# Rotary tables moved from the start into the compressed projections, vector loads on ACT's queue, the last squares summed by a second matmul

## The chip, the core and the metric

The kernel runs on one core of a Trainium2 chip. The metric is the device time of one execution in microseconds. The core has five instruction streams that run side by side and meet at semaphores: TensorE (PE, matmuls; its weight loads are listed as PEld), VectorE (DVE), ScalarE (ACT), GpSimd (POOL) and SyncE (SP), which here only issues transfers. Any of SP, ACT and POOL can issue a DMA; the transfers themselves run on the core's 16 DMA engines.

## What is computed

The reference is an encoder of two layers on 1024 tokens of width 1024. Cut to what the change touches:

```python
cos, sin = rope_tables(positions)         # angles positions * inv_freq: (1024, 16)
c_act = silu(c)
for l in range(2):
    mod = c_act @ w_ada[l] + b_ada[l]     # six rows of 1024: shift, scale, gate, twice
    h = rmsnorm(x, g_mix[l]) * (1 + scale_a) + shift_a
    proj = h @ w_in[l]                    # q_na, k_na, v_na, c_q, c_kv, k_rope, gates
    # neighbourhood attention on q_na, k_na, v_na
    # latent attention on c_q (256), c_kv (128), k_rope (32):
    #   q = rmsnorm(c_q) @ w_uq, its rotary part and k_rope turned by cos and sin
    x = x + gate_a * (merged @ w_out[l])
    h = rmsnorm(x, g_mlp[l]) * (1 + scale_m) + shift_m
    x = x + gate_m * (relu(h @ w_ff1[l]) ** 2 @ w_ff2[l])
return rmsnorm(x, g_final)
```

## The kernel before, in words

The activations lie transposed in SBUF, eight tiles of 128 channels by 1024 tokens, in two halves `ch` of 512 tokens. Every dense product is done as three matmuls: each operand is split into a rounded high part (a cast on ACT, line 201) and the rest (a subtraction on DVE, line 202), and the three products high x high, high x low and low x high add up in PSUM (lines 208 to 210, in the token projections 459 to 461).

The start goes as follows. SyncE loads `c`, the positions, the eight row tiles of `x` (line 132), seven parameter vectors as rows (`load_rows`, line 116), and then sixteen tiles of `w_ada` (line 160), eight for the scale and eight for the shift of layer 0. There are eight completion semaphores for transfers, which are used in turn, and a transfer's issue waits until the earlier one with the same semaphore has landed. DVE computes the rotary tables (lines 302 to 326: angle in turns, split into chunks, reduced modulo one by adding and subtracting a large number in `frac`, lines 309 and 310, and summed in halves at line 319); two sines on ACT (350, 351) finish them into `sinT` and `cosT`, and line 143 loads ACT's usual table again. ACT squares the rows of x (337), POOL makes each row's norm factor out of the sum (338, 339, a power) and a diagonal matrix `dg` of it (342). TensorE turns the rows by a matmul with `dg` (347), and ACT copies the normalised, turned tiles `yT` out (349). DVE sums the ada tiles weighted with `c_act` (line 169 for the first tile, 171 for the others) into `acc1` (scale) and `acc0` (shift). `turn_rows` (123, 124) turns the parameter vectors into columns `cols`; `ada_turn` (185 to 194) adds the sums' partitions up and makes `mod` and `amix`. With these, line 271 modulates `yT`, and after the split the projections begin.

The first projection makes the 416 compressed columns (`c_sink`, 474 to 492, one unit of 24 matmuls for each of eight token tiles) with the norms of `c_q` and `c_kv`; the second the 512 value columns, again eight units. Between value units TensorE does the rotary queries: `query_rot` (line 739) makes 128 tokens x 256 rotary columns `pqr`, `rotate` (380 to 392) turns them on DVE with `sinT` and `cosT` into `qrr`, and one unit later `query_turn` (751) transposes `qrr` on TensorE (756) into `pqrT`. Two token tiles are done after one unit. The scale row of the next modulation, `ada(0, 2)`, is also summed in this stage.

`square_sum` (233) adds up the squares of the eight output tiles while they are made, in the output projection of both layers and in the second product of the channel mixer: ACT squares, DVE adds to `sums`. `rstd_first` (243) sums over partitions with one fp32 matmul with a matrix of ones (245; the trace shows two instructions for it).

The Tile framework builds the program: a scheduler with a model of the engines sets each engine's order, only instructions in `tc.keep_in_program_order` keep theirs. PSUM tiles of one bank come from a pool of four; streamed tiles (`raw`) from a pool of three; `slab` tiles from an arena of 32.

Of the kernel before, what the change touches and what calls it, by code (L numbers as in the profile page):

```python
# [9 lines left out]
F32 = mybir.dt.float32  # L10
# [27 lines left out]
def hybrid_trunk(  # L38
# [42 lines left out]
    def slab(s, shape=(P, 1024), dt=F32):  # L81
        return arena.tile(list(shape), dt, tag="slab", name=nm(s))
# [28 lines left out]
    def load_rows(group, base):  # L111
        t = tmp("vrows", (P, P))
        n = 0
        for name, ap, cnt in group:
            flat = ap if len(ap.shape) == 1 else ap.rearrange("a b -> (a b)")
            nc.sync.dma_start(t[n:n + cnt, :], flat.rearrange("(r p) -> r p", p=P))
            col0[name] = base + n
            n += cnt
        return t, n
# [5 lines left out]

    tc_, nc_ = load_rows(rows_c, 248)
    pint = tmp("pi", (8, P), I32)
    nc.sync.dma_start(pint, positions.rearrange("a (i p) -> (a i) p", p=P))
    xrow = []
    for i in range(8):  # L130
        t = slab("xrow")
# [10 lines left out]
    def exp_ln_tables():  # L142
        tc.keep_in_program_order(A.preload_act_table_set("natural_log_exp_and_others"))
# [54 lines left out]
        nc.sync.dma_start(dst.bitcast(F32), src.bitcast(F32))  # L198

    def split(dst_hi, dst_lo, src, pin=lambda ins: ins):  # L200
        pin(A.copy(dst_hi, src))  # L201
        V.tensor_tensor(dst_lo, src, dst_hi.bitcast(F32), op=ALU.subtract)  # L202

    def mm3(ps, terms, first=True, **kw):

# [22 lines left out]

    pipe = Pipe()

    sums = [None, None]

    def square_sum(src, ch, n):

        if n == 0:
            sums[ch] = pool["ws"].tile([P, CH], F32, tag=f"sums{ch}", name=nm("sums"), bufs=1)
            A.activation(sums[ch], src, AF.Square)
        else:
            sq = tmp("sq")
            A.activation(sq, src, AF.Square)  # L240
            V.tensor_tensor(sums[ch], sums[ch], sq, op=ALU.add)

    def rstd_first(ch):
        ps = bank("pss")
        T.matmul(ps, ones, sums[ch], start=True, stop=True)
        v = tmp("var")
        V.tensor_scalar(v, ps, 1.0 / D, EPS, op0=ALU.mult, op1=ALU.add)
        r0 = tmp("r0")
        A.activation(r0, v, AF.Ln)
        A.activation(r0, r0, AF.Exp, scale=-0.5)  # L250
        return v, r0
# [43 lines left out]
        V.memset(invf[:, i:i + 1], f)  # L295

    dense_open()
    n, chunks, magic = P, turn_chunks(), 1.5 * 2.0 ** 23
    turns, rest = (pool["ws"].tile([P, 2048], F32, tag="ws", name=s) for s in ("turns", "rest"))
    ang, parts = rest[:, 1792:1920], rest[:, 1536:1792]  # L300
    for i in range(8):
        V.tensor_scalar(ang[:, i * 16:(i + 1) * 16], invf, posT[:, i:i + 1], None, op0=ALU.mult)
    ahi = parts[:, n:]
    V.tensor_copy(ahi.bitcast(F32R), ang)
    V.tensor_tensor(parts[:, :n], ang, ahi, op=ALU.subtract)

    def frac(t):
        w = rest[:, :t.shape[1]]
        V.tensor_scalar(w, t, magic, magic, op0=ALU.add, op1=ALU.subtract)
        V.tensor_tensor(t, t, w, op=ALU.subtract)  # L310

    m = 2 * n * len(chunks)
    for i, cval in enumerate(chunks):
        V.tensor_scalar(turns[:, 2 * n * i:2 * n * (i + 1)], parts, cval, None, op0=ALU.mult)
    frac(turns[:, :m])
    frac(turns[:, :m])
    while m > n:
        half = m // n // 2 * n
        V.tensor_tensor(turns[:, :half], turns[:, :half], turns[:, m - half:m], op=ALU.add)
        frac(turns[:, :half])  # L320
        m -= half
    two_pi = 2.0 * math.pi * (1 - 2.0 ** -22)
    flat = lambda t: t[:].rearrange("p a b -> p (a b)")
    turn, quarter = turns[:, :n], turns[:, n:2 * n]
    V.tensor_scalar(quarter, turn, 0.25, None, op0=ALU.add)
    frac(quarter)


    x_d = dram.tile([D, S], F32, name="x_d")
# [13 lines left out]
    for ch in range(2):  # L343
        for k in range(8):
# [2 lines left out]
                T.matmul(ps[:, i * P:(i + 1) * P], xrow[4 * ch + i][:, k * P:(k + 1) * P], dg[ch][:, i, :],  # L347
                         start=True, stop=True)
            A.copy(yT[k][:, cs(ch)], ps)
    tc.keep_in_program_order(A.activation(flat(sinT), turn, AF.Sin, scale=two_pi))  # L350
    tc.keep_in_program_order(A.activation(flat(cosT), quarter, AF.Sin, scale=two_pi))
    exp_ln_tables()
    pin = tc.keep_in_program_order
    ada_sum(acc1, first_scale, 0, pin)
    ada_sum(acc0, first_shift[:5], 0, pin)
    turn_rows(ta, na_, 0)
# [92 lines left out]
    def projections(l, h, xs, mla, extra, behind, early):  # L449
# [24 lines left out]
        def c_sink(i, ps):  # L474
# [12 lines left out]
                pipe.later(1, mla["key_copy"], ctok, i // 2)  # L487
            if i in (4, 5, 6, 7):
                vws.extend(token_weights(l, 1024, 512, [i - 4], pin=tc.keep_in_program_order))
            if i == 3:  # L490
                for k in range(8):
                    nc.sync.dma_start(x_d[k * P:(k + 1) * P, :], xs[k])
# [482 lines left out]
    def layer(l, xs, h, extra, behind, early):  # L975
# [61 lines left out]

        def operand_h(p, k, src):
            t = hq[p, k] = pair_slab("h")
            split(t[:, 0, :], t[:, 1, :], src)  # L1040

        def scaled(ch, r, ks):
            for k in ks:
# [462 lines left out]
def turn_chunks():  # L1506

    from fractions import Fraction

    digits = "0.1591549430918953357688837633725143620344596457404564487476673440588967976342265350901138027662530859560728"  # L1510
    rest = Fraction(digits)
    got = []
    for _ in range(6):
        e = math.floor(math.log2(float(rest)))
        step = Fraction(2) ** (e - 11)
        c = (rest / step).__floor__() * step
        got.append(float(c))
        rest -= c
    return got
# [26 lines left out]
```

## Time and profile before

| | us |
|---|---|
| median of 3 runs (3151.32 to 3154.35) | 3153.73 |
| the profiled execution | 3154.83 |
| its span, first to last instruction | 3153.0 |
| TensorE busy (96%) | 3033.6 |
| VectorE busy (66%) | 2069.4 |
| ScalarE busy (47%) | 1471.2 |
| GpSimd busy (12%) | 373.0 |

The shares are of the span. TensorE's mean granted clock is 0.988 of full speed. Matmuls are pipelined, so that a recorded duration overlaps the next; the step from start to start tells what one costs in a run of them. An "idle before" in a row is the time that the engine did nothing ahead of that instruction, and the name behind the arrow is what came last before it could start.

### The profile page before, as it was taken

Reading aid. Unit: us, or ns where it says so; the run is one execution under the profiler, and the core shown is the slowest. Engines: PE = TensorE matmul, PEld = TensorE weight load, DVE = VectorE, ACT = ScalarE, POOL = GpSimd, SP = SyncE. Lnnn points to the kernel's source line nnn. Section 1 sums busy time; section 2 is a strip of 40 time slices with the busy share of each in tenths; the row PEclk is TensorE's granted clock in tenths of the full one; section 3 lists DMA queues with packets and bytes.
Section 4 is the critical chain, followed back from the end, with each engine's and each line's share of the span. In section 5 each row is a group of like instructions: output and inputs, shape, how many; then the busy total and the mean of one; then the engine's idle time right before and its main releaser. Section 6 shows DMA issues by size and latency. Waiting matters only on the chain. (4 is left out here: it accounts for less than half of the span.)

```text
span 3153.0 us, 43333 instructions
## 1 busy us (share of the span) xinstructions
PE 3033.6 (96%) x15104; PEld 2456.0 (78%) x15104; DVE 2069.4 (66%) x3911; ACT 1471.2 (47%) x2820; POOL 373.0 (12%) x518
## 2 busy tenths in 40 slices
PE   7999999999998999999989999999999999999998
PEld 6878886776786888888777788777777778888887
DVE  8534436767859776877774334466775697767775
ACT  6234446554127666433352444555522466663332
POOL 5111002232200000000011011123221000000000
PEclk9999999999999999999999999999999999999999
DMA  6554334214853656856334444431266255586652
GB/s 258 157 135 111 99 109 119 63 36 145 280 191 107 244 207 231 293 196 209 106 121 138 125 121 114 117 86 36 73 214 218 69 180 214 211 308 205 215 166 84
DMA packets 359540, 497.56 MB, mean 158 GB/s; under 512 B 30556, under 2 KB 238618, under 8 KB 359322
## 3 DMA queue, kind: packets, MB, share of 16 engines
q1 hardware_dynamic: 359322, 494.80, 48.9%
q8 instruction: 119, 1.95, 0.3%
q14 instruction: 99, 0.81, 0.1%
HBM read 335.41 MB, written 141.98 MB: 151 GB/s over the span
## 5 line engine op out<-in xcount | busy, mean ns | idle before, releaser
L208 PE MATMUL pd<-h,wh 128*128 128x512 f32 x768 | 307.0, 400 | 0.6 <-ACT wh L201 0.6
L210 PE MATMUL pd<-h,wh 128*128 128x512 f32 x768 | 300.7, 392 | 0.0
L209 PE MATMUL pd<-h,wh 128*128 128x512 f32 x768 | 300.1, 391 | 0.0
L208 PE MATMUL pxz<-ho,wq 128*128 128x512 f32 x672 | 259.9, 392 | 3.5 <-DVE xT L1401 3.0
L209 PE MATMUL pxz<-ho,wq 128*128 128x512 f32 x672 | 261.8, 390 | 0.5 <-DVE ho L1153 0.5
L210 PE MATMUL pxz<-ho,wq 128*128 128x512 f32 x672 | 257.0, 389 | 0.0
L201 ACT CAST wq<-s 128x512 fp32r<-128x512 f32 (+3 forms) x296 | 154.5, 541 | 125.5 <-PE pxz L210 54.2
L208 PE MATMUL px<-h,wq 128*128 128x512 f32 x512 | 202.2, 396 | 3.5 <-ACT u L1242 2.3
L1401 DVE SCALAR_TENSOR_TENSOR xT<-pxz,mod,xT 128x512 f32<-128x512 f32 x252 | 186.7, 744 | 28.4 <-PE pxz L210 28.3
L798 DVE TENSOR_REDUCE sm<-smla 128x1 f32<-128x1024 f32 x128 | 156.6, 1223 | 69.7 <-PE smla L796 63.3
L209 PE MATMUL px<-h,wq 128*128 128x512 f32 x512 | 200.2, 392 | 1.4 <-DVE h L202 1.4
L210 PE MATMUL px<-h,wq 128*128 128x512 f32 x512 | 199.6, 391 | 0.0
L801 ACT ACTIVATE pmla<-smla,sm 128x1024 f32<-128x1024 f32 x128 | 143.0, 1117 | 118.2 <-DVE sm L799 113.3
L803 POOL TENSOR_SCALAR pmla<-pmla,sm 128x1024 f32<-128x1024 f32 x128 | 144.6, 1130 | 330.4 <-DVE sm L799 153.7
L202 DVE TENSOR_TENSOR wq<-s,wq 128x512 fp32r<-128x512 f32 (+3 forms) x296 | 168.7, 582 | 6.9 <-ACT wq L201 6.9
L796 PE MATMUL smla<-st,st 128*128 128x512 f32 x512 | 170.4, 413 | 2.9 <-ACT pmla L801 2.9
L208 PEld LDWEIGHTS pd<-h,wh 128*128 128x128 f32 x768 | 144.9, 189 | 32.4 <-issue 3.4
L210 PEld LDWEIGHTS pd<-h,wh 128*128 128x128 f32 x768 | 144.6, 188 | 32.8 <-issue 1.0
L209 PEld LDWEIGHTS pd<-h,wh 128*128 128x128 f32 x768 | 145.1, 189 | 28.3
L201 ACT CAST wq<-wr 128x384 fp32r<-128x384 f32 (+3 forms) x218 | 114.7, 539 | 106.2 <-PE pxz L210 62.6
L209 PE MATMUL pyz<-h,wq 128*128 128x512 f32 x384 | 151.6, 395 | 8.0 <-DVE h L202 8.0
L208 PEld LDWEIGHTS pxz<-ho,wq 128*128 128x128 f32 x672 | 126.1, 188 | 36.3 <-issue 4.8
(281 smaller groups left out, 7344.3 us busy)
## 6 DMA issues: line engine op xcount, KB each, us to landing
hid_d<-diff SPq DMA_DIRECT2D x112, 512.0 KB
ho<-hid_d SPq DMA_DIRECT2D x112, 512.0 KB
wada<-in_w_ada_dram SPq DMA_DIRECT2D x96, 512.0 KB
wr<-in_w_ff_dram SPq DMA_DIRECT2D x64, 512.0 KB
w<-in_w_in_dram SPq DMA_DIRECT2D x56, 512.0 KB
wr<-in_w_ff_dram SPq DMA_DIRECT2D x64, 384.0 KB
ho<-hid_d SPq DMA_DIRECT2D x84, 256.0 KB
hid_d<-u SPq DMA_DIRECT2D x68, 256.0 KB
```

The lines of the kernel that those rows point to most:

```text
L201: pin(A.copy(dst_hi, src))
L202: V.tensor_tensor(dst_lo, src, dst_hi.bitcast(F32), op=ALU.subtract)
L208: T.matmul(ps, wh, mh, start=first and i == 0, stop=False, **kw)
L209: T.matmul(ps, wh, ml, start=False, stop=False, **kw)
L210: T.matmul(ps, wl, mh, start=False, stop=i == n - 1, **kw)
L796: T.matmul(ps[:, cs(ch)], a[:, t], b[:, cs(ch)], start=i == 0, stop=i == 2)
L798: V.reduce_max(sm[:, 0:1], ps, axis=AX.X)
L801: A.activation(pt, ps, AF.Exp, bias=sm[:, 1:2], scale=MLA_SCALE, accum_out=sm[:, 2:3])
L803: G.tensor_scalar(pt, pt, sm[:, 3:4], 1.0, op0=ALU.mult, op1=ALU.mult)
L1401: V.scalar_tensor_tensor(x, ps, gate_m[:, nt:nt + 1], x, op0=ALU.mult, op1=ALU.add)
```

## The change

- The eight loads of vectors and the load of the positions are issued by ACT instead of SyncE.
- The rotary tables are computed in a function `rotary_tables()`, called in the first layer's compressed projection at its fifth unit instead of at the start. The work tiles are three slabs, and the chunks are worked in two halves of 768 columns instead of one of 1536. The first eight operations and the two sines keep their place in the program's order.
- In `square_sum` the last of the eight squares isn't added by DVE; `rstd_first` adds it by a second matmul into the same PSUM tile.
- `split` and `operand_h` return their instructions.

```diff
@@ -113,7 +113,7 @@
         n = 0
         for name, ap, cnt in group:
             flat = ap if len(ap.shape) == 1 else ap.rearrange("a b -> (a b)")
-            nc.sync.dma_start(t[n:n + cnt, :], flat.rearrange("(r p) -> r p", p=P))
+            nc.scalar.dma_start(t[n:n + cnt, :], flat.rearrange("(r p) -> r p", p=P))
@@ -125,7 +125,7 @@
 
     tc_, nc_ = load_rows(rows_c, 248)
     pint = tmp("pi", (8, P), I32)
-    nc.sync.dma_start(pint, positions.rearrange("a (i p) -> (a i) p", p=P))
+    nc.scalar.dma_start(pint, positions.rearrange("a (i p) -> (a i) p", p=P))
@@ -198,8 +198,8 @@
         nc.sync.dma_start(dst.bitcast(F32), src.bitcast(F32))
 
     def split(dst_hi, dst_lo, src, pin=lambda ins: ins):
-        pin(A.copy(dst_hi, src))
-        V.tensor_tensor(dst_lo, src, dst_hi.bitcast(F32), op=ALU.subtract)
+        a = pin(A.copy(dst_hi, src))
+        return a, V.tensor_tensor(dst_lo, src, dst_hi.bitcast(F32), op=ALU.subtract)
@@ -228,7 +228,7 @@
-    sums = [None, None]
+    sums, last_sq = [None, None], [None, None]
@@ -238,11 +238,15 @@
         else:
             sq = tmp("sq")
             A.activation(sq, src, AF.Square)
-            V.tensor_tensor(sums[ch], sums[ch], sq, op=ALU.add)
+            if n < 7:
+                V.tensor_tensor(sums[ch], sums[ch], sq, op=ALU.add)
+            else:
+                last_sq[ch] = sq
 
     def rstd_first(ch):
         ps = bank("pss")
-        T.matmul(ps, ones, sums[ch], start=True, stop=True)
+        T.matmul(ps, ones, sums[ch], start=True, stop=False)
+        T.matmul(ps, ones, last_sq[ch], start=False, stop=True)
         v = tmp("var")
         V.tensor_scalar(v, ps, 1.0 / D, EPS, op0=ALU.mult, op1=ALU.add)
         r0 = tmp("r0")
@@ -295,35 +299,45 @@
...
-    n, chunks, magic = P, turn_chunks(), 1.5 * 2.0 ** 23
-    turns, rest = (pool["ws"].tile([P, 2048], F32, tag="ws", name=s) for s in ("turns", "rest"))
-    ang, parts = rest[:, 1792:1920], rest[:, 1536:1792]
-    for i in range(8):
-        V.tensor_scalar(ang[:, i * 16:(i + 1) * 16], invf, posT[:, i:i + 1], None, op0=ALU.mult)
-    ahi = parts[:, n:]
-    V.tensor_copy(ahi.bitcast(F32R), ang)
-    V.tensor_tensor(parts[:, :n], ang, ahi, op=ALU.subtract)
-
-    def frac(t):
...
-    for i, cval in enumerate(chunks):
-        V.tensor_scalar(turns[:, 2 * n * i:2 * n * (i + 1)], parts, cval, None, op0=ALU.mult)
-    frac(turns[:, :m])
-    frac(turns[:, :m])
...
+    def rotary_tables():
+
+        n, chunks, magic = P, turn_chunks(), 1.5 * 2.0 ** 23
+        ta, tb, tw = (slab(s) for s in ("turns", "turns", "rest"))
+        parts, ang = tw[:, 768:1024], ta[:, 896:1024]
+        for i in range(8):
+            pin(V.tensor_scalar(ang[:, i * 16:(i + 1) * 16], invf, posT[:, i:i + 1], None, op0=ALU.mult))
+        ahi = parts[:, n:]
+        V.tensor_copy(ahi.bitcast(F32R), ang)
+        V.tensor_tensor(parts[:, :n], ang, ahi, op=ALU.subtract)
+
+        def frac(t):
+            w = tw[:, :t.shape[1]]
+            V.tensor_scalar(w, t, magic, magic, op0=ALU.add, op1=ALU.subtract)
+            V.tensor_tensor(t, t, w, op=ALU.subtract)
+
+        m = n * len(chunks)
+        for t, cut in ((ta, chunks[:len(chunks) // 2]), (tb, chunks[len(chunks) // 2:])):
+            for i, cval in enumerate(cut):
+                V.tensor_scalar(t[:, 2 * n * i:2 * n * (i + 1)], parts, cval, None, op0=ALU.mult)
+            frac(t[:, :m])
+            frac(t[:, :m])
+        V.tensor_tensor(ta[:, :m], ta[:, :m], tb[:, :m], op=ALU.add)
+        frac(ta[:, :m])
+        while m > n:
+            half = m // n // 2 * n
+            V.tensor_tensor(ta[:, :half], ta[:, :half], ta[:, m - half:m], op=ALU.add)
+            frac(ta[:, :half])
+            m -= half
+        two_pi = 2.0 * math.pi * (1 - 2.0 ** -22)
+        turn, quarter = ta[:, :n], ta[:, n:2 * n]
+        V.tensor_scalar(quarter, turn, 0.25, None, op0=ALU.add)
+        frac(quarter)
+        pin(A.activation(flat(sinT), turn, AF.Sin, scale=two_pi))
+        pin(A.activation(flat(cosT), quarter, AF.Sin, scale=two_pi))
+        exp_ln_tables()
...
@@ -347,10 +361,6 @@
                 T.matmul(ps[:, i * P:(i + 1) * P], xrow[4 * ch + i][:, k * P:(k + 1) * P], dg[ch][:, i, :],
                          start=True, stop=True)
             A.copy(yT[k][:, cs(ch)], ps)
-    tc.keep_in_program_order(A.activation(flat(sinT), turn, AF.Sin, scale=two_pi))
-    tc.keep_in_program_order(A.activation(flat(cosT), quarter, AF.Sin, scale=two_pi))
-    exp_ln_tables()
-    pin = tc.keep_in_program_order
     ada_sum(acc1, first_scale, 0, pin)
     ada_sum(acc0, first_shift[:5], 0, pin)
     turn_rows(ta, na_, 0)
@@ -487,6 +497,8 @@
                 pipe.later(1, mla["key_copy"], ctok, i // 2)
             if i in (4, 5, 6, 7):
                 vws.extend(token_weights(l, 1024, 512, [i - 4], pin=tc.keep_in_program_order))
+            if i == 4 and l == 0:
+                rotary_tables()
@@ -1037,7 +1049,7 @@
 
         def operand_h(p, k, src):
             t = hq[p, k] = pair_slab("h")
-            split(t[:, 0, :], t[:, 1, :], src)
```

DVE at the start, before: `ada_43` is the shift's sum, `ada_42` the scale's (its last row stands first), `cols` the turned vectors.

```order
L171 SCALAR_TENSOR_TENSOR ada_42_233<-wada_33_215,c_act_114,ada_42_233 128x1024
L169 TENSOR_SCALAR ada_43_234<-wada_34_217,c_act_114 128x1024
L171 SCALAR_TENSOR_TENSOR ada_43_234<-wada_35_219,c_act_114,ada_43_234 128x1024
L124 COPY cols_81<-pcols_62_382 128x112
L124 COPY cols_81<-pcols_63_385 128x62
L171 SCALAR_TENSOR_TENSOR ada_43_234<-wada_36_221,c_act_114,ada_43_234 128x1024
L187 TENSOR_REDUCE mod0_118<-pada_64_388 128x4
L187 TENSOR_REDUCE mod0_118<-pada_65_394 128x4
L171 SCALAR_TENSOR_TENSOR ada_43_234<-wada_37_223,c_act_114,ada_43_234 128x1024
L189 TENSOR_TENSOR mod0_118<-mod0_118,cols_81 128x8
L171 SCALAR_TENSOR_TENSOR ada_43_234<-wada_38_225,c_act_114,ada_43_234 128x1024
```

The same place after:

```order
L171 SCALAR_TENSOR_TENSOR ada_43_197<-wada_37_186,c_act_114,ada_43_197 128x1024
L171 SCALAR_TENSOR_TENSOR ada_43_197<-wada_38_188,c_act_114,ada_43_197 128x1024
L124 COPY cols_81<-pcols_62_342 128x112
L124 COPY cols_81<-pcols_63_345 128x62
L187 TENSOR_REDUCE mod0_118<-pada_64_348 128x4
L187 TENSOR_REDUCE mod0_118<-pada_65_354 128x4
L189 TENSOR_TENSOR mod0_118<-mod0_118,cols_81 128x8
L193 TENSOR_SCALAR amix0_120<-mod0_118 128x8
L194 TENSOR_TENSOR amix0_120<-amix0_120,cols_81 128x8
L171 SCALAR_TENSOR_TENSOR ada_43_197<-wada_39_190,c_act_114,ada_43_197 128x1024
L171 SCALAR_TENSOR_TENSOR ada_43_197<-wada_40_192,c_act_114,ada_43_197 128x1024
L171 SCALAR_TENSOR_TENSOR ada_43_197<-wada_41_194,c_act_114,ada_43_197 128x1024
```

Of the shift's eight sums two stood ahead of the copies into `cols` before, and five do now; the other three stand together behind `amix`.

DVE in the value projections, before, at the second token tile's rotation (`pqr_181` into `qrr_182`; `pqr_177` and `qrr_178` are the first's); `ada_250` is the next modulation row's sum.

```order
L391 TENSOR_TENSOR qrr_178_1124<-pqr_177_1117,cosT_124 128x8x16
L386 TENSOR_TENSOR rot_183_1141<-pqr_181_1133,sinT_125 128x128
L171 SCALAR_TENSOR_TENSOR ada_250_1563<-wada_255_1576,c_act_114,ada_250_1563 128x1024
L387 TENSOR_TENSOR qrr_182_1140<-pqr_181_1133,cosT_124 128x8x16
L388 TENSOR_TENSOR qrr_178_1124<-qrr_178_1124,rot_179_1125 128x8x16
L392 TENSOR_TENSOR qrr_178_1124<-qrr_178_1124,rot_180_1129 128x8x16
L390 TENSOR_TENSOR rot_184_1145<-pqr_181_1133,sinT_125 128x128
L391 TENSOR_TENSOR qrr_182_1140<-pqr_181_1133,cosT_124 128x8x16
L171 SCALAR_TENSOR_TENSOR ada_250_1563<-wada_256_1579,c_act_114,ada_250_1563 128x1024
L388 TENSOR_TENSOR qrr_182_1140<-qrr_182_1140,rot_183_1141 128x8x16
L392 TENSOR_TENSOR qrr_182_1140<-qrr_182_1140,rot_184_1145 128x8x16
```

The same engine after, up to the first token tile's rotation (`pqr_180` into `qrr_181`); `turns_146` and `rest_148` are the tables' work tiles, `ada_253` the same modulation row.

```order
L171 SCALAR_TENSOR_TENSOR ada_253_1568<-wada_261_1590,c_act_114,ada_253_1568 128x1024
L316 TENSOR_TENSOR turns_146_802<-turns_146_802,rest_148_804 128x384
L328 TENSOR_TENSOR turns_146_802<-turns_146_802 128x128
L315 TENSOR_SCALAR rest_148_804<-turns_146_802 128x128
L316 TENSOR_TENSOR turns_146_802<-turns_146_802,rest_148_804 128x128
L328 TENSOR_TENSOR turns_146_802<-turns_146_802 128x128
L315 TENSOR_SCALAR rest_148_804<-turns_146_802 128x128
L316 TENSOR_TENSOR turns_146_802<-turns_146_802,rest_148_804 128x128
L333 TENSOR_SCALAR turns_146_802<-turns_146_802 128x128
L315 TENSOR_SCALAR rest_148_804<-turns_146_802 128x128
L396 TENSOR_TENSOR rot_182_1130<-pqr_180_1122,sinT_125 128x128
L316 TENSOR_TENSOR turns_146_802<-turns_146_802,rest_148_804 128x128
```

Six of the eight sums stood ahead of the end of the second tile's rotation before; now all eight stand ahead of the first tile's, and so does the rest of the tables, of which only the last addition stands behind the first operation on `pqr`.

ACT's queue at the start, before:

```order
L149 ACT_TABLE_LOAD
L149 ACTIVATE csig<-cols 128x8 [waits DVE_49]
L337 ACTIVATE yT_193,xss<-xrow_86 128x1024 [waits DMAHW2_49]
L337 ACTIVATE yT_194,xss<-xrow_88 128x1024 [waits DMAHW3_49]
L337 ACTIVATE yT_195,xss<-xrow_90 128x1024 [waits DMAHW4_49]
```

And after, from the third of its nine loads on; `DMAHW1`, `DMAHW3` and so on are completion semaphores of transfers.

```order
L116 DMA vrows_102<-in_b_ada_dram 96x128
L116 DMA vrows_102<-in_g_mix_dram 16x128
L116 DMA vrows_105<-in_g_mlp_dram 16x128 [waits DMAHW1_49]
L116 DMA vrows_105<-in_g_final_dram 8x128 [waits DMAHW3_49]
L116 DMA vrows_105<-in_b_gate_dram 32x128 [waits DMAHW5_49]
L116 DMA vrows_105<-in_g_q_dram 4x128 [waits DMAHW7_49]
L116 DMA vrows_105<-in_g_kv_dram 2x128 [waits DMAHW1_49]
L149 ACT_TABLE_LOAD
L149 ACTIVATE csig<-cols 128x8 [waits DVE_49]
L351 ACTIVATE yT_156,xss<-xrow_86 128x1024
L351 ACTIVATE yT_157,xss<-xrow_88 128x1024 [waits DMAHW2_49]
```

Nine loads stand ahead of the first table load now. The fifth, `g_mlp`, waits for the semaphore of the first row of x, the last, `g_kv`, for that of `g_mlp`.

## Rows read from the trace of the kernel before

**Rows 1.** The page, part 1: busy us, share of the span, x instructions.
```profile
PE 3033.6 (96%) x15104; PEld 2456.0 (78%) x15104; DVE 2069.4 (66%) x3911; ACT 1471.2 (47%) x2820; POOL 373.0 (12%) x518
```

**Rows 2.** Busy us by stretch, PE to POOL; PE clock, DMA share, GB/s.
```profile
15.00:16.00 1.00, 1.00 (x5) 0.75 (x4) 0.93 (x3) 0.85 (x1) 0.92 (x2) 1.00 0.00 0
55.00:107.00 52.00, 51.50 (x265) 48.29 (x264) 37.33 (x87) 24.87 (x76) 24.72 (x39) 0.97 0.47 163
81.65:117.74 36.09, 33.35 (x172) 29.47 (x171) 27.61 (x75) 13.74 (x44) 7.16 (x16) 1.00 0.60 189
82.40:83.70 1.30, 1.30 (x8) 1.28 (x8) 0.11 (x1) 1.30 (x5) 1.08 (x3) 1.00 0.33 100
```

**Rows 3.** Time line of the start: start, us, engine and operation [idle before].
```profile
1.51 3.76 SPq L132 DMA_DIRECT2D xrow<-in_x_dram  x8
...
2.35 0.24 PE L123 MATMUL pcols<-ident,vrows 8*128 8x8 f32 x1 [2.35 <-DMA vrows<-in_c_dram]
...
5.23 1.06 ACT L337 ACTIVATE yT<-xrow 128x1024 f32<-128x1024 f32 x1 [2.19 <-DMA xrow<-in_x_dram]
...
15.14 13.95 SPq L160 DMA_DIRECT2D wada<-in_w_ada_dram  x16
```

**Rows 4.** Time line of DVE at the start.
```profile
3.93 1.20 DVE L302 TENSOR_SCALAR rest<-invf,posT 128x16 f32<-128x16 f32 x8
...
7.08 0.96 DVE L309 TENSOR_SCALAR rest<-turns 128x1536 f32<-128x1536 f32 x1
...
12.72 0.96 DVE L319 TENSOR_TENSOR turns<-turns 128x768 f32<-128x768 f32 x1
...
13.71 0.62 DVE L309 TENSOR_SCALAR rest<-turns 128x768 f32<-128x768 f32 x1
...
15.36 0.56 DVE L319 TENSOR_TENSOR turns<-turns 128x384 f32<-128x384 f32 x1
...
19.71 0.75 DVE L169 TENSOR_SCALAR ada<-wada,c_act 128x1024 f32<-128x1024 f32 x1
...
22.50 7.89 DVE L171 SCALAR_TENSOR_TENSOR ada<-wada,c_act,ada 128x1024 f32<-128x1024 f32 x6 [0.38 <-DVE ada L171]
```

**Rows 5.** Time line of POOL, the power of the row norms.
```profile
19.35 0.55 POOL L339 TENSOR_TENSOR xss<-xss,mhalf 128x1 f32<-128x1 f32 x1
...
20.94 1.59 POOL L339 TENSOR_TENSOR xss<-xss,mhalf 128x1 f32<-128x1 f32 x1
```

**Rows 6.** Time line of 28 to 46 us.
```profile
28.05 8.37 PE L347 MATMUL pyT<-dg,xrow 128*128 128x128 f32 x58 [2.15 <-POOL dg L342]
...
37.06 1.28 ACT L350 ACT_TABLE_LOAD   x1
...
42.08 3.92 DVE L171 SCALAR_TENSOR_TENSOR ada<-wada,c_act,ada 128x1024 f32<-128x1024 f32 x3
```

**Rows 7.** Time line of the first query rotations.
```profile
103.99 0.75 DVE L169 TENSOR_SCALAR ada<-wada,c_act 128x1024 f32<-128x1024 f32 x1 [2.08 <-DMA wada<-in_w_ada_dram]
...
117.46 0.28 DVE L392 TENSOR_TENSOR qrr<-qrr,rot 128x128 f32<-128x128 f32 x1
...
117.89 0.66 PE L756 MATMUL pqrT<-ident,qrr 128*128 128x128 f32 x2 [1.87 <-DVE qrr L392]
```

**Rows 8.** Time line of a norm that TensorE waits for.
```profile
951.53 0.63 ACT L240 ACTIVATE sq<-xT 128x512 f32<-128x512 f32 x1 [1.16 <-DVE xT L1028]
...
952.62 0.69 DVE L241 TENSOR_TENSOR sums<-sums,sq 128x512 f32<-128x512 f32 x1
...
953.36 1.59 PE L245 MATMUL pss<-sums,ones 128*128 128x512 f32 x2 [2.65 <-DVE sums L241]
```

**Rows 9.** Account of line 245: what its engine waited for before it.
```profile
  DVE sums L241: 17.6, 6
```

**Rows 10.** Time line of PE at a norm without a wait.
```profile
933.32 1.02 PE L245 MATMUL pss<-sums,ones 128*128 128x512 f32 x2
933.78 0.80 PE L208 MATMUL pd<-m,ws 128*128 128x512 f32 x1
```

More of the change, by code (lines that the diff above doesn't have):

```diff
@@ L297, in hybrid_trunk @@
     dense_open()
-    n, chunks, magic = P, turn_chunks(), 1.5 * 2.0 ** 23
-    turns, rest = (pool["ws"].tile([P, 2048], F32, tag="ws", name=s) for s in ("turns", "rest"))
-    ang, parts = rest[:, 1792:1920], rest[:, 1536:1792]
-    for i in range(8):
-        V.tensor_scalar(ang[:, i * 16:(i + 1) * 16], invf, posT[:, i:i + 1], None, op0=ALU.mult)
-    ahi = parts[:, n:]
-    V.tensor_copy(ahi.bitcast(F32R), ang)
-    V.tensor_tensor(parts[:, :n], ang, ahi, op=ALU.subtract)
-    def frac(t):
-        w = rest[:, :t.shape[1]]
-        V.tensor_scalar(w, t, magic, magic, op0=ALU.add, op1=ALU.subtract)
-        V.tensor_tensor(t, t, w, op=ALU.subtract)
@@ L312, in hybrid_trunk @@
-    m = 2 * n * len(chunks)
-    for i, cval in enumerate(chunks):
-        V.tensor_scalar(turns[:, 2 * n * i:2 * n * (i + 1)], parts, cval, None, op0=ALU.mult)
-    frac(turns[:, :m])
-    frac(turns[:, :m])
[L317 to L322, printed above, removed]
+    def rotary_tables():
[31 more added lines that the diff above has]
+        exp_ln_tables()
@@ L323, in hybrid_trunk @@
     flat = lambda t: t[:].rearrange("p a b -> p (a b)")
-    turn, quarter = turns[:, :n], turns[:, n:2 * n]
-    V.tensor_scalar(quarter, turn, 0.25, None, op0=ALU.add)
-    frac(quarter)
+    pin = tc.keep_in_program_order
     x_d = dram.tile([D, S], F32, name="x_d")
@@ L1039, in operand_h @@
             t = hq[p, k] = pair_slab("h")
-            split(t[:, 0, :], t[:, 1, :], src)
+            return split(t[:, 0, :], t[:, 1, :], src)
         def scaled(ch, r, ks):
```

## Prediction

> **What bounds the kernel now.** I read the page first: TensorE (PE) is busy for 3033.6 of 3153.0 us [rows 1], so little but an idle TensorE can be won, and every new idle stretch of it is paid in full. Then the busy times by stretch: from 55 to 107 us PE works 51.50 of 52 us while VectorE (DVE) works 37.33 [rows 2], so in the projections DVE has slack, if the work fits into it. Last I read the time line at the three places that the change touches: the start, the query rotation in the value projections, and the norms after the output projection.
>
> At the start the path to the first projection runs over the ada sums. SyncE issues the first `wada` load at 15.14 us, after 8 rows of x and all vectors, each of which waits for an earlier transfer [rows 3]; the DMA engines move nothing between 15 and 16 us [rows 2]. DVE computes the rotary tables from 3.93 us, and comes to the first sum at 19.71, when the load has just landed; the sums then follow at 7.89 / 6 = 1.315 us each [rows 4]. The last three of the shift's sums start at 42.08 and end at 46.0 [rows 6]. Beside it POOL makes the row norms `dg`: its power costs 0.55 us alone and 1.59 us beside DVE's sums [rows 5], and the last `dg` releases 8.37 us of TensorE work at 28.05, up to 36.4 [rows 6]. The copies of the vectors into `cols`, in DVE's queue ahead of the remaining sums, wait for that.
>
> **Part 1, the start: -3.0 us.** Two edits act here. Without the vectors SyncE issues x at once: two issues earlier, at 3.76 / 8 = 0.47 us each [rows 3], some 0.8 us in all, and the first `wada` follows x with no transfer of a vector between. The empty microsecond and its surroundings close, so the first `wada` lands at an estimated 15.6 us (19.5 less 0.8 and less some 3 us of gap and small transfers). DVE has nothing else then and can sum from 15.6 on: 13 sums are ahead of the copies into `cols`, 13 x 1.315 = 17.1, done at 32.7.
>
> But the copies wait for TensorE, which waits for POOL, and POOL for ACT's squares. ACT now issues nine loads ahead of its first table load. The fifth waits for the first row of x (landed at 5.23 before [rows 3], 4.4 now), the ninth for the fifth; a vector took from 0.72 to 2.35 us, 1.6 us, to land (the row of 2.35 [rows 3]), so the ninth issues at some 6.5, and with the table load of 1.28 us [rows 6] the squares start at 8.2 to 8.4 instead of 5.23. At 1.27 us each, five of eight are done when the sums begin, and POOL does the last three rows, nine instructions, beside the sums at 1.4 each (between 1.05 and 1.59): 16.0 + 12.6 = 28.6, against 28.0 before. I take 28.0 to 28.6 as no shift. So TensorE turns the vectors as before, at 36.4, and what changes is behind it: three sums instead of six. Copies to 37.0, the two reductions and three small operations (some 2.1 us, no longer covered by sums between them), then 3 x 1.31 = 3.9: the shift is done at 43.0 instead of 46.0. The weights' casts, the modulation and the first projection hang on it and shift by the same 3.0. Bounds: POOL free of contention would give its last `dg` at 19.7, and the sums alone would end at 32.7 + 2.1 + 3.9 + 0.3 = 39.0, a gain of 7.0; the other end is the second rival, a loss of 3.0.
>
> The Trainium skill, page SBUF — State Buffer, section Who interferes with whom, says that a DVE instruction with two SBUF inputs contends with a GpSimd instruction that reads SBUF. The sums have two such inputs, and the 0.55 against 1.59 us of [rows 5] agree; the rule speaks against this edit, since sums that start earlier meet more of POOL's rows. By the rule the gain is the 3.0 us above, without it it would be the 7.0.
>
> **Part 2, the tables in the projections: +11.4 us.** What is removed from the start stood before the sums and is paid in part 1. What is added: the same arithmetic in halves of 768. By wall time it was 19.71 - 3.93 = 15.78 us; its two reductions modulo one at 1536 took from 7.08 to 12.72, 5.64 us; four at 768 take 15.36 - 13.71 = 1.65 each, 6.6 [rows 4]. So 16.7 us if all stand one behind the other, and some 2.6 less, 14.1, if other work stands between the 25 of them that use what the one before made (an estimate of 0.1 us for each such hand-over). I take 15, as most have neighbours from the projections. The order of the changed kernel shows where it ends: the last of it, and all eight sums of the next ada row, two more than before, stand ahead of the first query rotation.
>
> From 81.65 us to the end of the second query rotation, 117.46 + 0.28 = 117.74 [rows 7], DVE has 27.61 us of work in 36.09 [rows 2]. In the changed kernel: 27.6, plus 15, plus two sums at 1.2 = 2.4, plus idle time that stays because the work next in the queue isn't ready: 1.3 at 82.4, where DVE does 0.11 [rows 2], and 0.8 of the 2.08 before the first sum, which waits for its load [rows 7]; 47.1 us, so 128.8. The 6.3 us of other idle time are filled; that is all the cover there is. To this comes the round trip to ACT for the cosine, 0.4: DVE's second operation on the query waits for the last reduction, the activation (0.3) and two hand-overs. In all 129.1 or 11.4 later. PE waited 1.87 us for this rotation before [rows 7] and has nothing else in its order until it has it, so it waits 11.4 longer, and since it is busy to the end of the stage and beyond, nothing gives it back. Bounds: 14.1 and all idle filled, 8; 16.7, every idle time kept as it is (8.5 instead of 2.1), 19.4. ACT's two table loads at 1.28 and two sines leave the time from 37 to 40 us, where DVE's sums are what ends last [rows 6], and return in this stall, where ACT has no other work: nothing either way.
>
> **Part 3, the last squares: -0.5 us.** At six places the sum of squares is turned by one fp32 product more and one DVE addition less. In three of them, as at 953, PE sits idle 2.65 us for DVE: the last square is done at 951.53 + 0.63 = 952.16, the addition ends at 952.62 + 0.69 = 953.31 [rows 8], so the product can start 1.15 earlier. That there are three such places the account of this line tells: six times, 17.6 us in all, TensorE stood idle before it until DVE was done, which is its products and its weight loads at three places [rows 9]. An additional pair costs 0.46, the step from 933.32 to 933.78 at a place where nothing waits [rows 10]; behind an idle stretch I take 0.5. So 3 x (1.15 - 0.5) = 1.95 is gained. At the other three, PE does not idle and pays 3 x 0.46 = 1.4. Both together make 0.5. Bounds: the extra pair twice as long at the three, 3 x (1.15 - 1.2) - 1.4 = -1.6; hidden in the three, 3.45 - 1.4 = +2.1.
>
> The new return values change no instruction here: 0.
>
> **Sum.** -3.0 + 11.4 - 0.5 = +7.9. The profiled execution took 3154.83 us, 1.1 above the median; it would become 3162.7, and from the median of 3153.73 the forecast is **3161.6**.
>
> **Rivals.** (A) The tables do fit into DVE's slack. For it: DVE is idle for 14.7 us between 55 and 107 [rows 2]. Against it: the stage in which the tables are due offers 8.5. It decides if the second rotation ends before 121 us: then the stall grows by 3 or less, and the time is 3153.73 - 3.0 + 3 - 0.5 = 3153.2, or 3150.2 with none: not slower. Chance 0.2.
> (B) ACT's queue holds the squares back. If the waits among its nine loads let the squares start at 10.5, POOL has fifteen instructions left when the sums begin, its last `dg` comes at some 34, when the sums are through and it is alone again, the vectors are turned at 42.4, and the shift is done at 49: 3.0 lost instead of won. 3153.73 + 3.0 + 11.4 - 0.5 = 3167.6. For it: the fifth and ninth load wait for landings. Chance 0.15.
> (C) The move of the vectors doesn't bring the ada rows forward, as all transfers share the same engines: first `wada` at 18.7, only the 0.8 earlier. Then POOL meets fewer sums, its last `dg` comes at some 23, the 13 sums end at 18.7 + 17.1 = 35.8, and 2.1 + 3.9 behind them give 41.9, a gain of 4.1: 3160.5. Chance 0.15.
>
> **How the numbers follow.** The forecast has 0.5; its own range, from a rotation of 8 to 16 and a start of 1 to 6, is 3156 to 3167. What this kernel's measurement can tell from no change is 0.2%, 6.3 us: 3147.4 to 3160.0. The forecast is slower in 0.31, same in 0.18, faster in 0.01; A same in 0.14, faster in 0.06; B slower in 0.15; C slower in 0.08, same in 0.06, faster in 0.01. Together faster 0.08, same 0.38, slower 0.54. The range from 3149 to 3168 holds A's lower case and B's price, and leaves out a start that gains its 7.0 together with A, and the 19.4.
>
> **What would show it.** In the changed kernel: first sum on DVE at 15 to 16 us (C: 18.7); first square on ACT at 8.4 (B: past 10); shift done at 43; PE idle in front of the second query transposes 10 to 14 us, with DVE's reductions and sums without a gap before it (A: under 5); the product over `sums` at 953 about 1.1 us after its last square and not 1.2 before. Wrong I would be if the stall stayed under 5 us, or if the three norm places gained more than a microsecond each.

## The result, and the profile after

The changed kernel takes 3173.14 us (median of 4 runs, 3166.7 to 3173.5) where the kernel before takes 3153.46 beside it: ratio 1.0059, 95% interval 1.0041 to 1.0076, 19.7 us slower. Run again later it was 1.0048 [1.0036, 1.0061], 15.3 us. The forecast was 3161.6, 7.9 slower, and its range ended at 3168: the direction is right, the size is less than half of what it is.

The profiled execution of the changed kernel took 3166.7 us, 11.9 more than that of before. The page says that TensorE has no more to do: 3035.2 us against 3033.6 [rows 1], for twelve instructions more. So nearly all of the loss, 10.3 of the span's 11.9 us, is idle TensorE.

The page's part 1 after (busy us, share of the span, x instructions):

```profile
PE 3035.2 (96%) x15116; PEld 2456.6 (78%) x15116; DVE 2069.3 (65%) x3909; ACT 1470.7 (46%) x2820; POOL 377.5 (12%) x518
```

To find where, I paired TensorE's matmuls of the two profiles in order and looked how far each is behind its counterpart, in us from the start of its own span. The first projection is 0.3 us late (55.47 against 55.19), the first transposes of the compressed tokens 3.4 (74.49 against 71.14), the stretch before 107 us 5.4, and what follows the query rotation 18.3. From there to layer 1 it is between 16 and 21. In the projections of layer 1 this one execution makes up some 7 us. The execution profiled again is 19.5 behind at 140 us, up to 28 before layer 1's projections, and ends 20.5 behind. So a loss of the measured size stands before 140 us, in two waits and in what stands behind them; what later stages add and give back differs between executions.

Time line of TensorE after, rows with a wait (start, us, operation, [idle before <- releaser]):

```profile
55.47 0.46 PE L469 MATMUL ptok<-ws,h 128*128 128x416 f32 x1 [0.84 <-ACT h L201]
...
74.49 0.66 PE L672 MATMUL pcT<-ident,ctok 128*128 128x128 f32 x2 [5.14 <-DVE ctok L493]
...
117.66 0.50 PE L469 MATMUL ptok<-ws,h 128*128 128x512 f32 x1 [3.21 <-DVE cg L676]
...
135.74 1.16 PE L768 MATMUL pqrT<-ident,qrr 128*128 128x128 f32 x4 [10.70 <-DVE qrr L402]
```

The last row answers to the rotation's of [rows 7]: the transposes of both rotations now follow one wait of 10.70, where two stood, 1.02 and 1.87. The third row, 3.21, had no counterpart. The same view of the kernel before has the first transposes (`pcT`) and the first rotation's:

```profile
71.14 0.44 PE L660 MATMUL pcT<-ident,ctok 128*128 128x128 f32 x2 [0.50 <-DVE ctok L483]
...
115.58 0.44 PE L756 MATMUL pqrT<-ident,qrr 128*128 128x128 f32 x2 [1.02 <-DVE qrr L392]
```

The start after, all engines:

```profile
4.67 0.32 ACTq L116 DMA_DIRECT2D vrows<-in_g_mlp_dram  x1
...
9.17 0.24 ACTq L116 DMA_DIRECT2D vrows<-in_g_kv_dram  x1
9.45 1.28 ACT L149 ACT_TABLE_LOAD   x1 [9.45 <-DMA vrows<-in_g_final_dram]
...
10.86 1.04 ACT L351 ACTIVATE yT<-xrow 128x1024 f32<-128x1024 f32 x1
...
15.48 0.75 DVE L169 TENSOR_SCALAR ada<-wada,c_act 128x1024 f32<-128x1024 f32 x1 [4.33 <-DMA wada<-in_w_ada_dram]
...
19.75 1.52 POOL L353 TENSOR_TENSOR xss<-xss,mhalf 128x1 f32<-128x1 f32 x1
...
32.67 8.73 PE L361 MATMUL pyT<-dg,xrow 128*128 128x128 f32 x58 [1.85 <-POOL dg L356]
...
44.15 3.92 DVE L171 SCALAR_TENSOR_TENSOR ada<-wada,c_act,ada 128x1024 f32<-128x1024 f32 x3
```

ACT issues its ninth load at 9.17 and the first square at 10.86; before it was 5.23 [rows 3]. DVE's first sum is at 15.48, before 19.71 [rows 4]. POOL's power costs 1.52 beside the sums, as in [rows 5]; its last run of `dg` releases TensorE at 32.67, 4.6 us later than in [rows 6], and the shift is done at 44.15 + 3.92 = 48.07, 2.1 later than in [rows 6].

Stretches of the changed kernel (busy us PE, PEld, DVE, ACT, POOL; TensorE's clock, DMA share, GB/s), and two of the kernel before:

```profile
74.49:78.50 4.01, 4.01 (x14) 3.87 (x15) 1.14 (x5) 0.00 (x0) 2.10 (x5) 0.58 0.00 0
86.87:114.40 27.53, 27.30 (x144) 24.57 (x143) 23.06 (x64) 11.17 (x36) 12.23 (x16) 1.00 0.43 126
114.40:136.08 21.68, 7.77 (x27) 5.86 (x26) 20.75 (x49) 5.44 (x11) 0.00 (x0) 0.76 0.78 228
119.00:122.10 3.10, 3.10 (x9) 2.41 (x8) 3.10 (x8) 2.10 (x4) 0.00 (x0) 0.50 1.04 328
135.70:137.70 2.00, 1.96 (x9) 1.79 (x10) 1.13 (x4) 0.74 (x2) 0.00 (x0) 0.50 0.34 131
```

```profile
71.14:73.60 2.46, 2.46 (x14) 2.44 (x15) 1.19 (x4) 0.24 (x1) 0.95 (x3) 1.00 0.00 0
117.80:119.80 2.00, 1.91 (x9) 1.94 (x10) 1.80 (x3) 0.37 (x1) 0.00 (x0) 0.50 0.87 244
```

From 114.40 to the end of the second rotation DVE has no slack left, 20.75 of 21.68 us, and TensorE works 7.77. The clock column, the granted share of full speed, has the rest of the price: behind the 5.14 us of idling it is 0.58 for 4 us where it was 1.00 before, and behind the 3.21 us it is 0.50, the lower level of 1.2 GHz, for 3.1 us. Behind the rotation it was 0.50 before as well, so there it costs nothing new.

DVE at the end of the stage, the tables' chain (L315, L316, L328) between the sums of the next ada row (L171), then the rotations:

```profile
128.52 1.28 DVE L171 SCALAR_TENSOR_TENSOR ada<-wada,c_act,ada 128x1024 f32<-128x1024 f32 x1
129.72 0.55 DVE L316 TENSOR_TENSOR turns<-turns,rest 128x384 f32<-128x384 f32 x1
130.31 0.29 DVE L328 TENSOR_TENSOR turns<-turns 128x128 f32<-128x128 f32 x1
...
133.40 0.29 DVE L397 TENSOR_TENSOR qrr<-pqr,cosT 128x128 f32<-128x128 f32 x1 [0.38 <-ACT cosT L336]
...
135.80 0.28 DVE L402 TENSOR_TENSOR qrr<-qrr,rot 128x128 f32<-128x128 f32 x1
```

### The profile page after: what moved, and what is told of

It reads as the page before. It is cut to its first block, busy times and chain, and to the rows that moved or that the text cites. A ratio compares the mean times of both kernels' runs of the same rounds, so it can differ in the third digit from the quotient of the medians.

```text
span 3164.9 us, 43356 instructions
## 1 busy us (share of the span) xinstructions
PE 3035.2 (96%) x15116; PEld 2456.6 (78%) x15116; DVE 2069.3 (65%) x3909; ACT 1470.7 (46%) x2820; POOL 377.5 (12%) x518
```

## The experiments

Three pairs of theories were open. Is it the tables in DVE's queue, or the start? Why are the first transposes late? And do the last squares win anything? Each time below stands beside that of the kernel before, run with it.

| kernel | ratio [95%] | us against before |
|---|---|---|
| tables moved alone | 1.0041 [1.0027, 1.0054] | +14.6 |
| vector loads moved alone | 1.0011 [1.0002, 1.0020] | +4.3 |
| last squares alone | 1.0010 [1.0001, 1.0019] | +3.3 |
| the changed kernel again | 1.0048 [1.0036, 1.0061] | +15.3 |
| whole ada row in the output stage | 1.0135 [1.0121, 1.0149] | +41.9 |
| tables at the stage's start | 1.0046 [1.0033, 1.0060] | +13.4 |
| five vector loads behind the squares | 1.0069 [1.0057, 1.0082] | +21.8 |
| ada row later and loads behind | 1.0153 [1.0138, 1.0168] | +47.8 |
| whole ada row behind the rotation | 1.0052 [1.0038, 1.0066] | +17.7 |
| tables alone, early, ada row behind | 1.0025 [1.0015, 1.0035] | +8.4 |
| the same, modulation shared out | 1.0012 [1.0001, 1.0024] | +3.9 |
| before, modulation shared out | 0.9989 [0.9978, 1.0000] | -3.1 |

**The three parts, each alone.** The kernel before with only `rotary_tables()` moved to the token loop (`if i == 4 and l == 0`), with only `nc.sync` turned to `nc.scalar` in the vectors' loads, and with only the last square given to a second product.

> The kernel before with the rotary tables moved into the compressed projections, and nothing else of the change. Theory 1 (the move carries the loss, by two stalls of TensorE: about 5 us in front of the first transposes of the compressed projection, since the first three token units are interleaved and evicted together, and about 13 us at the first query rotation; the start gains 3 us since ACT squares early and POOL is through before DVE's sums begin): 3164 to 3172 us. Rival (the loss comes from the vector loads, which hold ACT's squares back): at most 3160 us.

> The kernel before with the nine vector loads issued by ACT, and nothing else of the change. Theory 1: the squares start at 10.5 to 11 us instead of 5.2, POOL's last diagonal comes at 31 to 33 instead of 28 us, the first projection starts 1 to 5 us later: 3154 to 3159 us. Rival: 3160 us and more.

> The kernel before with the last squares summed by a second matmul, and nothing else of the change. Theory 1: a gain of 0.3 to 0.7 us at three places, a loss of 0.46 at three, 3151 to 3155 us. Rival (the earlier product keeps TensorE's clock up behind it): 3148 to 3151 us.

> The changed kernel once more, on the same chip as its three parts. Theory 1: the parts add up, and the time is 3171 to 3175 us, as in three of its four executions; its profile shows again 13 us more at the first query rotation and 5 at the first transposes. Rival: 3166 to 3168 us, as in the profiled execution, with layer 1's projections 7 us shorter.

The tables alone carry nearly all of it. The start, without the loads on ACT's queue:

```profile
16.82 0.38 POOL L352 TENSOR_SCALAR dg<-ident,xss 128x128 f32<-128x128 f32 x1
...
18.37 0.75 DVE L169 TENSOR_SCALAR ada<-wada,c_act 128x1024 f32<-128x1024 f32 x1 [14.37 <-DMA wada<-in_w_ada_dram]
...
38.96 3.92 DVE L171 SCALAR_TENSOR_TENSOR ada<-wada,c_act,ada 128x1024 f32<-128x1024 f32 x3
```

POOL is through at 17.2 us, before the first sum, with 0.55 us for each of its powers, and the shift is done at 38.96 + 3.92 = 42.9, 3.1 earlier than before. The Trainium skill, page SBUF — State Buffer, section Who interferes with whom, says that two-input DVE instructions contend with GpSimd's reads; the pair of 0.55 here and 1.52 beside the sums agrees. But the gain does not last. TensorE in the same kernel:

```profile
71.10 0.66 PE L668 MATMUL pcT<-ident,ctok 128*128 128x128 f32 x2 [5.71 <-DVE ctok L489]
...
132.71 1.16 PE L764 MATMUL pqrT<-ident,qrr 128*128 128x128 f32 x4 [11.94 <-DVE qrr L398]
```

It reaches the first transposes 5.2 us early and waits 5.71 for `ctok`; the row stands at 71.10, before at 71.14. So a shift that comes earlier is worth nothing there. What sets that place is POOL's twelve modulated tiles and, behind them, DVE's `ctok` copies: POOL takes 18.3 us for the twelve in each of the four kernels, from 49.44 before, from 48.15 here (of the shift's 3.1 us 1.3 are left, as DVE has the subtraction of a weight tile, at 45.55, ahead of the reduction to `mod`), and in the changed kernel:

```profile
51.52 18.35 POOL L275 TENSOR_SCALAR yT<-yT,amix,mod 128x512 f32<-128x512 f32 x12 [18.89 <-DVE mod L189]
```

In the order of the changed kernel the first three token units are interleaved to their end and DVE's copies of `ctok` stand behind all the subtractions of their operands (from 71.16 on). Before, the first copy, at 68.21, stood ahead of the last subtraction, at 68.72. This order comes with the tables' move and not with the loads' or the squares'. With it the transposes come 4.6 us behind the end of POOL's tiles, here and in the changed kernel, where it was 3.4; these 1.2 take back the 1.3 here. Against this kernel the changed one is 3.4 us late at the transposes (74.49 against 71.10) and 3.0 behind the rotation (135.74 against 132.71): the price of the loads.

The loads alone keep the tables ahead of the sums and put the squares at 10.72:

```profile
9.04 0.24 ACTq L116 DMA_DIRECT2D vrows<-in_g_kv_dram  x1
...
10.72 1.04 ACT L337 ACTIVATE yT<-xrow 128x1024 f32<-128x1024 f32 x1
```

POOL's twelve tiles then start at 56.30 and the first projection at 62.5, 7.3 late. This execution makes that up only on the way, the last 4.5 us in layer 1's projections. Its +4.3 is uncertain (0.6 to 6.3).

The last squares alone, at the norm of [rows 8]:

```profile
958.43 0.63 ACT L240 ACTIVATE sq<-xT 128x512 f32<-128x512 f32 x1 [0.77 <-DVE xT L1032]
...
958.91 0.68 DVE L242 TENSOR_TENSOR sums<-sums,sq 128x512 f32<-128x512 f32 x1
...
959.65 1.13 PE L248 MATMUL pss<-sums,ones 128*128 128x512 f32 x2 [2.04 <-DVE sums L242]
...
960.62 1.02 PE L249 MATMUL pss<-sq,ones 128*128 128x512 f32 x2
```

The first product starts 0.59 us after its last square, where 1.2 stood before, but not at once: its releaser is the addition *before* the last (958.91 + 0.68 = 959.59), which stands in DVE's queue behind an operand's subtraction. So the wait goes from 2.65 to 2.04, by 0.61 and not by 1.15. And the added product is dearer than [rows 10] had it. The matmul behind the two of [rows 10], and the same place here:

```profile
934.42 0.40 PE L209 MATMUL pd<-m,ws 128*128 128x512 f32 x1
```

```profile
939.36 1.02 PE L248 MATMUL pss<-sums,ones 128*128 128x512 f32 x2
940.22 1.02 PE L249 MATMUL pss<-sq,ones 128*128 128x512 f32 x2
940.68 0.79 PE L208 MATMUL pd<-m,ws 128*128 128x512 f32 x1
941.31 0.40 PE L209 MATMUL pd<-m,ws 128*128 128x512 f32 x1
```

One pair goes by in 0.46 us, but the matmul after it then takes 0.64 (933.78 to 934.42), where a step is 0.23 otherwise. Two pairs take 1.32, so the added one costs 0.86 and not 0.46. At 959 too it costs more than the 0.61 that the wait gives back: from the last matmul ahead of the products to the first behind them it is 3.85 us where it was 3.64. Of the other two waits one falls by 0.60 and one by 0.10. An estimate from these steps is 6 x 0.86 less 1.3, some 3.9 us lost and nothing won anywhere; the measured +3.3 (0.3 to 6.0), outside the expectation, is of this size. The next wait of this norm, for the operand that the norm scales, also grows, from 4.31 to 4.91. Where TensorE's clock falls behind these waits differs between executions, and what that is worth is not separated here.

**Is it the queue on DVE?** If the rotation waits for what stands ahead of it on DVE, fewer sums there shorten it one for one. The whole ada row, eight sums, is moved to the output stage, in both layers.

```diff
-            if i < 6:
-                ada(l, {0: 2, 1: 4, 3: 3, 5: 5}[i])
+            if 0 < i < 6:
+                if i == 1:
+                    ada(l, 2)
+                ada(l, {1: 4, 3: 3, 5: 5}[i])
```

> The changed kernel, with the eight sums of the next modulation row moved from the value projections to the output stage (beside the row that is summed there already). Theory 1 (the stall at the first query rotation is DVE's queue: all that stands in it is paid): the sums are 0.67 + 7 x 1.2 = 9.1 us of that queue, TensorE's wait of 10.7 to 13.1 us in front of the query transposes falls to 2 to 5, and the time to 3159 to 3163 us. Rival (the stall is the tables' own chain of dependent operations and the sums only fill its gaps): the wait stays above 8 us, 3167 us and more.

```profile
126.81 1.16 PE L768 MATMUL pqrT<-ident,qrr 128*128 128x128 f32 x4 [4.72 <-DVE qrr L402]
...
809.57 1.97 PE L185 MATMUL pada<-ident,ada 128*128 128x128 f32 x8 [16.41 <-DVE ada L171]
```

The rotation's wait fell from 10.70 to 4.72 and the one of 3.21 is gone, together 9.2 us for the 9.1 that the eight sums were to take: the queue is the cause. But in the output stage two rows now stand one behind the other, and TensorE waits for the second in both layers, 16.41 us here and 16.7 in layer 1. The price was moved and more than doubled.

**Do the tables fit into the stage's first half?** `if i == 0 and l == 0` instead of `i == 4`.

> The changed kernel, with the tables called at the first unit of the compressed projection instead of the fifth. Theory 1: DVE stands idle between 70 and 88 us for some 7 us, which the tables can now use: the wait in front of the query transposes falls by 4 to 7 us, 3162 to 3167 us. Rival (the idle time there is the norms' round trips, which come later if DVE has other work): the gain is under 2 us, 3168 us and more.

```profile
74.59 0.66 PE L672 MATMUL pcT<-ident,ctok 128*128 128x128 f32 x2 [3.56 <-DVE ctok L493]
...
131.28 1.16 PE L768 MATMUL pqrT<-ident,qrr 128*128 128x128 f32 x4 [6.36 <-DVE qrr L402]
```

4.3 us of the second wait are gone, as DVE's slack in the first projection [rows 2] is used, and by 140 us the kernel is 13.9 behind, not 18.3. The wait falls as expected (by 4 to 7), the time does not: it gains 1.9 on the changed kernel run again, within the noise, and is 3169.05 where 3162 to 3167 was expected.

**Is ACT's queue what holds the squares?** `load_rows(rows_b, 128)`, five of the nine loads, is moved behind the loop of squares.

> The changed kernel, with the five smaller vector loads issued by ACT behind its squares instead of ahead of its first table load. Theory 1 (the waits among the nine loads hold the squares back, so that POOL meets DVE's sums): the squares start at 5 to 6 us instead of 10.9, POOL's last diagonal comes at 17 to 22 instead of 32.6, the shift is done at 41 to 43 instead of 48.1, and the first transposes of the compressed projection come 4 to 6 us earlier: 3164 to 3167 us. Rival (the start is hidden behind POOL's modulation, whatever the squares do): under 2 us, 3168 us and more.

```profile
4.45 1.06 ACT L350 ACTIVATE yT<-xrow 128x1024 f32<-128x1024 f32 x1 [0.45 <-DMA xrow<-in_x_dram]
...
16.68 1.17 POOL L355 TENSOR_SCALAR dg<-ident,xss 128x128 f32<-128x128 f32 x1
25.28 0.32 ACTq L116 DMA_DIRECT2D vrows<-in_g_mlp_dram  x1
...
30.71 2.05 ACT L363 COPY yT<-pyT 128x512 f32<-128x512 f32 x4 [15.85 <-DMA vrows<-in_g_final_dram]
...
31.34 13.10 PE L361 MATMUL pyT<-dg,xrow 128*128 128x128 f32 x96 [18.11 <-ACT yT L363]
```

The squares start at 4.45 and POOL is through at 17.9, but the expectation fails: a load in ACT's stream whose wait isn't over holds the copies behind it. ACT's first moved load is issued at 25.28, the copies that free TensorE's banks come at 30.71, and TensorE waits 18.11. Both edits together:

> The changed kernel with both, the sums of the next modulation row later and the five loads behind the squares. Theory 1: the two gains add up, 3154 to 3158 us, no slower than the kernel before. Rival: what the start gains is waited for again at the query rotation, where DVE's queue ends when it ends: 3159 us and more.

The wait at the rotation is 4.73 and at the ada row 16.49: the two prices add, not the two gains that were expected.

**The whole ada row behind the rotation.** The last addition of layer 0's second rotation and the sums of `ada(0, 2)` are kept in program order (`pin`), so that all eight sums stand behind.

> The changed kernel, with the eight sums of the next modulation row kept behind the second query rotation in DVE's order, in the same stage. Theory 1 (DVE's queue): the wait in front of the query transposes falls from 10.7 to 4 to 5 us as when the sums were two stages later, the one of 3 us in the unit before goes, and nothing comes back later, since the row is needed only in the output stage: 3158 to 3163 us. Rival (the sums only filled gaps of the tables' chain): 3167 us and more.

```profile
125.59 1.16 PE L769 MATMUL pqrT<-ident,qrr 128*128 128x128 f32 x4 [4.73 <-DVE qrr L402]
...
166.23 1.94 PE L185 MATMUL pada<-ident,ada 128*128 128x128 f32 x8 [5.36 <-DVE ada L171]
...
221.69 0.80 PE L208 MATMUL pd<-h,wh 128*128 128x512 f32 x1 [4.59 <-ACT wh L201]
```

After the rotation it is 8.2 behind, not 18.3; then the ada row and the weight casts come late, 5.36 and 4.59, and it is 17 behind at 250 us, where the changed kernel is 18. So the expectation that nothing comes back later failed: in this stage DVE has no room for the sums, ahead of the rotation or behind it.

**Are there versions without the losses?** Tables alone, early, sums behind; then also every second modulated tile given to DVE in both halves of the tokens, which shortens POOL's run; and this edit alone on the kernel before.

```diff
-            modulate(..., V if ch == 0 and k % 2 else G)
+            modulate(..., V if k % 2 else G)
```

> Tables in the compressed projection from its first unit on, the eight sums behind the second query rotation, vector loads and norms as in the kernel before. Theory 1: the first transposes come at 71 us as in the kernel before, the query transposes wait 1 to 4 us instead of 10.7 to 13, so little more than in the kernel before: 3154 to 3159 us. Rival (the move costs DVE time that TensorE waits for somewhere in any case): 3162 us and more.

> As the kernel with early tables and late sums, and four of POOL's twelve modulated tiles given to DVE. Theory 1 (between the shift and the first transposes the path is POOL's twelve tiles, 18.3 us): POOL is through some 5 us earlier, the first transposes come 3 to 5 us earlier, and the time falls below that of the kernel without this by as much: 3149 to 3155 us. Rival (DVE has no room there, and the subtractions for the operands come later instead): no gain.

> The kernel before, with four of POOL's twelve modulated tiles given to DVE, and nothing of the change. Theory 1: TensorE waits for POOL's end only 0.5 us there in the kernel before, so that at most 1 us can be won: 3152 to 3156 us. Rival: the operands come earlier and the first units run closer together, 3150 us and less.

```profile
71.18 0.66 PE L668 MATMUL pcT<-ident,ctok 128*128 128x128 f32 x2 [4.14 <-DVE ctok L489]
...
157.22 1.94 PE L185 MATMUL pada<-ident,ada 128*128 128x128 f32 x8 [5.23 <-DVE ada L171]
```

The first transposes are at 71.18 and no wait is left at the rotation, whose transposes are at 118.45, 0.6 behind the second ones of [rows 7]. Then it waits 5.23 for the ada row and 5.33 for a cast, is 10 behind at 250 us and 12 at the end, so that here too DVE's time is waited for elsewhere, as the rival had it. With the modulation shared out (eight tiles on POOL, 10.77 us instead of 18.3) the wait at the transposes falls to 0.67, but they come at 72.30 and not the expected 3 to 5 us earlier: TensorE now waits 2.69 for an operand of DVE at 56.18. The waits at 156 and 212 us (5.62 and 4.33) stay. The modulation alone, on the kernel before,

```profile
50.24 10.77 POOL L271 TENSOR_SCALAR yT<-yT,amix,mod 128x512 f32<-128x512 f32 x8 [22.49 <-ACT xT L368]
```

takes 3152.37 against 3155.43: -3.1 us with an interval from -6.9 to 0. It is the only kernel with a median below that of the kernel before, and barely told from no change. Nor does its trace show the gain at the tiles: there the first transposes come at 74.33, 3.2 later than before, behind a wait of 1.43 for an operand and a clock of 0.68 from 54 to 63 us, and what it gains it gains from layer 1's projections on.

## Why the prediction was right in direction and short in size

**Start, -3.0 predicted.** The step that failed: "the squares start at 8.2 to 8.4", and from it "28.0 to 28.6 as no shift". The squares start at 10.86, POOL's last `dg` releases TensorE at 32.67, the shift is done at 48.07: 2.1 lost, not 3.0 won. The first sum, 15.6 predicted, is at 15.48, so rival C is out. What was mis-sized is the landing of a vector: I took 1.6 us, what the vector of `c` took at the very start, from 0.72 to 2.35; the ninth load waits for the fifth, issued at 4.67, and goes out at 9.17, 4.5 us later, while the rows of x are on the way. This is rival B, with its point (10.5) and nearly its price (49). And only one of the two edits gains here: with the tables alone, and the vectors still on SyncE, the shift is 3.1 earlier, as POOL is through before the sums begin; the loads turn that into 2.1 later.

**What I didn't see.** I valued the shift's end as if the first projection carried it on. It doesn't: the first projection was only 0.3 late, and with a shift 3.1 earlier (tables alone) the transposes stood where they were. Between them lie POOL's twelve tiles, which I had no term for, and an order of the token units that the tables' move changes at a distance. POOL's tiles start 2.1 late and the new order adds 1.2: 3.4 us late at the transposes. The wait there is longer, 5.14 where 0.50 stood, because TensorE came earlier: its clock was 1.00 from 54 to 60 us, and 0.72 before. Behind the wait 1.7 us go to the lower clock (0.58 for 4 us), and it is 5.4 late by 107.

**Tables, +11.4 predicted.** Right as a mechanism: DVE's queue is full to the rotation, and taking sums out of it shortens the wait. In the time of before, the second rotation ends at 136.08 - 5.4 = 130.7, predicted 129.1. The waits are 3.21 + 10.70 - 1.02 - 1.87 = 11.0 more by these rows, and the clock's fall between the two, which I had no term for, makes 3.1 us at half speed, 1.6: together 12.6, beside the measured step from 5.4 to 18.3, 12.9.

**Last squares, -0.5 predicted.** The term that was mis-sized is the added pair: 0.46 to 0.5 predicted, 0.86 measured, as the step of [rows 10] leaves out what the matmul behind it loses. And the first product comes 0.6 earlier at two places and 0.1 at the third, not 1.15, as it now waits for the addition before. So each place loses by these steps. Alone it measured +3.3.

**Sum.** In place of -3.0 + 11.4 - 0.5 = 7.9 the runs show 5.4 by 107 us, 12.9 in the tables and some 3 in the squares, 21 to 22; the whole measures 15 to 20, with intervals from 11 to 24. The range kept its upper end at rival B with nothing else amiss; B came true, its loss grew at a join that it didn't count, and tables and squares were dearer as well.

**Open.** The parts measured alone add to 14.6 + 4.3 + 3.3 = 22, the whole measures 15 to 20, inside their intervals. Layer 1's projections differ by several us between executions (the changed kernel makes up 7 there in its first profile); I don't know why.

## What to carry to other kernels

Follow a gain to the next join before it is counted: an earlier start is worth nothing where TensorE then waits for an engine that started no earlier. An engine that is 66% busy over the span can have no slack in the one stage that matters; what was put there here was paid again, in part or more than doubled, wherever its neighbours were pushed. An instruction stream that issues loads is a queue like any other: count what stands behind each load that has to wait.

## What the runs showed of the hardware

A load in ACT's stream that waits for an earlier transfer stops ACT's computing until it may go: the first square came at 10.86 instead of 5.23, and a copy that TensorE needed at 30.71. Behind 5.1 us of idling TensorE's clock was 0.58 for 4 us, behind 3.2 us it was 0.50 for 3. POOL's 128x1 power took 0.55 us beside an idle DVE (seven of the eight with the tables alone, 0.56 the first) and 1.52 beside its two-input sums (the changed kernel). An added fp32 product with the matrix of ones, two instructions, cost 0.86 us where the clock column has 1.00 (939.36 to 940.68 for two products, 0.46 for one).
